# Hybrid decoder layer on one core: tile addresses at equal residues, and the order of five small steps

## The chip, the cores and the metric

One core of a Trainium2 chip runs the whole layer. The metric is the device time of one execution in microseconds (us). TensorE (PE) multiplies; VectorE (DVE), ScalarE (ACT) and GpSimd (POOL) compute; SyncE (SP), ACT and POOL also issue DMAs. Each engine takes its own instructions strictly in order.

## The reference

The input x has 1024 rows of 1024 float32. With h = RMSNorm(x)·g, one projection z = h·W_in (1024 x 6160) gives all branch inputs:

```
a_out = chunked_sgu(gelu(a_u), gelu(a_v), ...) * silu(a_gate)   # 8 groups of 128 channels
o     = gla_chunked(b_q, b_k, b_v, log_sigmoid(gate)/16)        # 4 heads, chunks of 64 rows
b_out = rmsnorm(o, per head) * silu(b_gate)
y     = concat(a_out, b_out) @ w_out                            # 2048 x 1024
return x + rmsnorm(y, post_g)
```

chunked_sgu normalizes its v over 1024 channels, multiplies each 128-row chunk by a lower triangular 128x128 matrix per group, adds a bias and multiplies by u.

## The kernel before

**Matrix products.** Every float32 operand of a large product is split into a rounded part hi and the rest lo (`split`, L104: a cast on ACT, a subtraction on DVE), and `mm3` (L108) makes three matmuls of each product: hi·hi, hi·lo, lo·hi. A matmul has a stationary operand of 128x128 and a moving one of 128x512 (128x256 in the attention). Two forms use the normalized, transposed h (tiles `hT`) and the weight granules (tiles `gr`): `proj_tok` (L170) moves the weights past a stationary piece of hT, in the trace `ps<-gr,hT`; `proj_col` (L180) moves hT past a stationary piece of weights, `ps<-hT,gr`. The output projection (`product`, L719) moves weights past the split left operands `ah` and `al`: `ps<-gr,ah`.

**Stages, in order of time.** (1) x is loaded, normalized and transposed by `prep` (L215) tile by tile, while `first_block` projects head 0's v and gate. (2) For the four heads, `qk` makes decayed q and k, and `attend` (L425 on) runs the gated linear attention by 128 rows. What follows an attend is put off by `later(fn, n)` and run at the n-th `tick` (one each 12 matmuls of a projection); so `out` (transposes of the finished og, L467, and its store to `mix_d`) stands with n = 3. (3) The first half and then the second half of a_v are projected and passed through Gelu and statistics (loop L543). Between the halves stand the transposes of the triangular matrices (L556), their copies `wsT` (L557) and their row sums (L562, a product with ones). (4) For 8 groups g: u and gate by `proj_col`, the spatial product (L589), and sums of W_out blocks by `wout_sums` (written to `wo_d`). (5) The output projection as seven products of halves (L764 to L799); the last one calls `done` for the post norm, the residual and the stores.

**What sets the order.** Tiles and waits come from a tile framework, which also orders each engine's instructions by a simulated timeline when the program is built; an edit in one place can shift neighbours. A pool hands out its buffers in turn and packs its tiles one behind the other, so a small tile shifts the start of all behind it.

**Addresses.** In the built program the byte address of each operand modulo 256 is the same for all matmuls of a kind: hT 224, gr 160, ah and al 160, attention v, st, qs and kst 96, sc 192, ident 128, h 160, wsT 224.

**Names.** `raw`: weights as loaded; `gain`: pre norm weights on all partitions, here made by two matmuls of ones with the row (L247 to L250); `first_a`: a part of mix_d read back for stage 5; `wb`, `wh`: the blocks of `wout_sums`.

Of the kernel before, what the change touches and what calls it, by code (L numbers as in the profile page):

```python
# [8 lines left out]
F32 = mybir.dt.float32  # L9
# [6 lines left out]
P = 128  # L16
# [17 lines left out]
def hybrid_layer(  # L34
# [55 lines left out]
    make_identity(nc, ident)  # L90
    neghalf = const.tile([P, 8], F32, name="neghalf")
    nc.vector.memset(neghalf, -0.5)

    def rsqrt(dst, mean, more=None):
        if more is None:
            nc.gpsimd.tensor_scalar(out=dst, in0=mean, scalar1=EPS, scalar2=None, op0=ALU.add)
        else:
            nc.vector.tensor_scalar(
                out=dst, in0=mean, scalar1=EPS, scalar2=more, op0=ALU.add, op1=ALU.add
            )  # L100
        nc.gpsimd.tensor_tensor(out=dst, in0=dst, in1=neghalf[:, : dst.shape[-1]], op=ALU.pow)
# [22 lines left out]

    def block_a(cols, before=lambda k2: None, fine=False):

        got = []
        for k2 in range(KT // 2):
            before(k2)
            raw = raw_tile([2, W])  # L130
            c = 0
            for c0, n in cols:
                nc.sync.dma_start(
                    raw[:, :, c : c + n],
                    w_in[k2 * 256 : (k2 + 1) * 256, c0 : c0 + n].rearrange("(k p) c -> p k c", p=P),
                )
                c += n
            hi, lo = granule([2, W])
            if fine:
                for j in range(2):  # L140
                    split(hi[:, j], lo[:, j], raw[:, j])
            else:
                split(hi, lo, raw)
            got += [(hi[:, j], lo[:, j]) for j in range(2)]
        return got

    def block_b(cols):
# [58 lines left out]
    with tc.tile_pool(name="pre", bufs=2) as pre:  # L206
# [45 lines left out]
        blk = block_a(  # L252
            ((C_BV, DV), (C_BG, DV)), lambda k2: load(1) if k2 == 2 else None, fine=True
        )
# [19 lines left out]
    with tc.tile_pool(name="gla", bufs=1) as gp:  # L274
# [21 lines left out]
        )  # L296
        ba = gp.tile([P, H], F32, name="ba")
        nc.gpsimd.dma_start(ba, b_a2.rearrange("(h p) -> p h", p=P))
# [35 lines left out]
        def gates(hd, hf):  # L334
# [36 lines left out]
            nc.scalar.activation(out=f, in_=f, func=AF.Exp, scale=1.0 / TAU)  # L371
            dec = gp.tile([P, 8, 1], F32, tag="dec", name="dec", bufs=2)
            nc.vector.tensor_copy(dec, b[:, :, CH - 1 : CH])
            dec2 = gp.tile([P, 4, 1], F32, tag="dec2", name="dec2", bufs=3)
            tt(out=dec2, in0=dec[:, 0::2], in1=dec[:, 1::2], op=ALU.mult)
# [49 lines left out]
        def attend(hd, t, got, v, sg, cur):  # L425
# [23 lines left out]
            if e == 0:  # L449
                cur["og"] = gp.tile([P, 2, DV], F32, tag="og", name="og", bufs=2)  # L450
                cur["oss"] = gp.tile([P, 2], F32, tag="oss", name="oss", bufs=2)
            og, oss = cur["og"], cur["oss"]
# [4 lines left out]
            if e == 1:  # L457
# [19 lines left out]

                later(out, 3)

# [39 lines left out]
    vn = [vnp.tile([P, NT, 256], F32, name=f"vn{j}") for j in range(4)]  # L519
    first_a = vnp.tile([P, 4, 4, P], F32, name="first_a")  # L520

    def mixed_a(g, hf):
        return vn[g // 2][:, 4 * hf : 4 * hf + 4, (g % 2) * P : (g % 2 + 1) * P]

    with tc.tile_pool(name="sgu", bufs=1) as sp_:
# [9 lines left out]
        )  # L535
        gb = sp_.tile([P, 2, G], F32, name="gb")
        nc.gpsimd.dma_start(gb[:, 0], ln_g.rearrange("(g p) -> p g", p=P))
# [5 lines left out]
        for i in range(2):  # L543
            if i == 1:
                blk = block_a(((C_V + 512, 512),))
            for t in range(NT):
                pv = pv_first[t] if i == 0 and t < 2 else proj_tok((t,), blk)[0]
                for j in range(2):
                    vt = vn[2 * i + j][:, t]
                    nc.scalar.activation(out=vt, in_=pv[:, j * 256 : (j + 1) * 256], func=AF.Gelu)  # L550
                    nc.vector.bn_stats(out=stats[:, t, 2 * i + j], in_=vt)
            if i == 0:
                for r in range(2):
                    pt = bank()
                    for g in range(4):
                        nc.tensor.transpose(pt[:, g * P : (g + 1) * P], wsr[:, 4 * r + g], ident)  # L556
                    nc.scalar.copy(  # L557
                        out=wsT[:, 4 * r : 4 * r + 4], in_=pt.rearrange("p (g c) -> p g c", g=4)
                    )
                for r in range(2):  # L560
                    pt = bank()
                    nc.tensor.matmul(  # L562
                        pt, ones, wsT[:, 4 * r : 4 * r + 4].rearrange("p g t -> p (g t)"),
                        start=True, stop=True,
                    )
                    for g in range(4 * r, 4 * r + 4):
                        nc.vector.scalar_tensor_tensor(
                            out=q[:, g], in0=pt[:, (g % 4) * P : (g % 4 + 1) * P],
                            scalar=gb[:, 1, g : g + 1], in1=q[:, g], op0=ALU.mult, op1=ALU.add,
                        )  # L570
        mv = sp_.tile([P, NT, 2], F32, name="mv")
        for t in range(NT):
            nc.vector.bn_aggr(out=mv[:, t], in_=stats[:, t].rearrange("p a b -> p (a b)"))
        rs = sp_.tile([P, NT, 1], F32, name="rs")
        rsqrt(rs.rearrange("p t o -> p (t o)"), mv[:, :, 1])
# [47 lines left out]
        for g in range(G):  # L623
# [7 lines left out]
            for i, func in enumerate((AF.Gelu, AF.Silu)):  # L631
                for hf in range(2):
# [28 lines left out]
    with tc.tile_pool(name="outp", bufs=1, side="right", reuse_waits="tile") as op:  # L661
        vtt = nc.vector.tensor_tensor
        pog = op.tile([P, D], F32, name="pog")
        nc.gpsimd.dma_start(pog, row_bc(post_g, D))
# [79 lines left out]
        y = [[op.tile([P, D], F32, name=f"y{hf}{t}") for t in range(4)] for hf in range(2)]  # L744
        sums = op.tile([P, 2, 4, 2], F32, name="sums")
        ss = [[sums[:, hf, t] for t in range(4)] for hf in range(2)]

# [5 lines left out]
        def finish(hf, t, xr, pieces):  # L753
            r = slice((4 * hf + t) * P, (4 * hf + t + 1) * P)
            rstd = op.tile([P, 1], F32, tag="rstd", name="rstd", bufs=2)
            rsqrt(rstd, ss[hf][t][:, 0:1], ss[hf][t][:, 1:2])
# [68 lines left out]
```

## Time and profile before

| | us |
|---|---|
| median of 3 runs (lowest, highest) | 813.18 (812.63, 816.85) |
| the profiled execution | 816.81 |
| its span, first to last instruction | 815.1 |
| PE busy in it | 786.8 (97%) |
| DVE, ACT, POOL busy | 415.6, 328.6, 129.2 |
| mean granted TensorE clock | 0.989 |

The page's line per engine gives busy time and share of the span. A busy PE is not a fast PE: a matmul's shown duration overlaps the next one's, so the pace is read from the distance between two starts. The granted clock is 1.0 at 2.4 GHz and 0.5 at 1.2 GHz. Idle time on an engine other than PE costs nothing unless PE waits for it.

### The profile page before, as it was taken

To read this page: it belongs to the slowest core of one execution; us is meant where nothing else is said; L and a number is where in the kernel's file an instruction comes from. 1 tells how busy PE (TensorE), PEld (TensorE's weight loads), DVE (VectorE), ACT (ScalarE), POOL (GpSimd) and SP (SyncE) were. 2 spreads that over 40 slices of the span, in tenths; PEclk is the share of its full clock that TensorE was granted. 3 is DMA by queue.
4 is the path that set the end of the run, shared out by engine and by line. 5 is a ranking of instruction groups with operands and counts; after the bars stand their busy time and mean duration, and the time that the engine had idled before them with its cause. 6 is when DMAs were issued, how large, how long until landed. Compare 5 with 4: busy or idle time off the path is not lost.

```text
span 815.1 us, 9989 instructions
## 1 busy us (share of the span) xinstructions
PE 786.8 (97%) x3776; PEld 644.6 (79%) x3776; DVE 415.6 (51%) x703; ACT 328.6 (40%) x589; POOL 129.2 (16%) x182
## 2 busy tenths in 40 slices
PE   5999999999899999999979999999999989999995
PEld 3888887888788878888858888888888878888884
DVE  5534589425552456252465586513333268534665
ACT  5536467326442644241333333323233243444431
POOL 1232234312321222112001011100000010000012
PEclk9999999999999999999989999999999999999998
DMA  9304011103010401034584765731110096344157
GB/s 282 115 2 116 4 50 53 52 27 110 27 52 2 136 27 52 1 124 136 207 257 169 222 218 192 243 119 52 53 53 27 26 358 261 132 154 153 52 188 276
DMA packets 62946, 97.33 MB, mean 119 GB/s; under 512 B 4849, under 2 KB 38641, under 8 KB 62898
## 3 DMA queue, kind: packets, MB, share of 16 engines
q1 hardware_dynamic: 54816, 68.76, 25.9%
q0 software_dynamic: 7504, 27.41, 9.5%
q8 instruction: 30, 0.49, 0.2%
q10 hardware_dynamic: 578, 0.53, 0.2%
q14 instruction: 18, 0.15, 0.1%
HBM read 71.51 MB, written 25.17 MB: 119 GB/s over the span
## 4 chain that ended last, share of the span: by engine, by line
PE 81%; DVE 5%; ACT 5%; DMA 4%; issue 3%; POOL 1%; SPq 0%; POOLq 0%; DVEq 0%; ACTq 0%
PE ps L111 25%; PE ps L112 25%; PE ps L113 25%; PE ps L589 2%; DMA raw<-in_w_in_dram 2%; ACT gr L105 1%; PE ps L321 1%; DMA wo_d<-wb 1%; PE ps L236 1%; DMA wsr<-in_a_w_s_dram 1%; PE ps L467 1%; DVE stl L106 1%; DVE b L355 1%; DVE og L460 1%; DVE y L758 1%
## 5 line engine op out<-in xcount | busy, mean ns | idle before, releaser
L111 PE MATMUL ps<-gr,hT 128*128 128x512 f32 x384 | 154.7, 405 | 0.0
L112 PE MATMUL ps<-gr,hT 128*128 128x512 f32 x384 | 152.9, 399 | 0.0
L113 PE MATMUL ps<-gr,hT 128*128 128x512 f32 x384 | 152.3, 398 | 0.0
L111 PE MATMUL ps<-hT,gr 128*128 128x512 f32 x384 | 152.2, 396 | 0.0
L113 PE MATMUL ps<-hT,gr 128*128 128x512 f32 x384 | 151.6, 396 | 0.0
L112 PE MATMUL ps<-hT,gr 128*128 128x512 f32 x384 | 151.4, 394 | 0.0
L106 DVE TENSOR_TENSOR gr<-raw,gr 128x1024 fp32r<-128x1024 f32 (+1 forms) x64 | 73.3, 1154 | 33.8 <-ACT gr L105 33.8
L111 PE MATMUL ps<-gr,ah 128*128 128x512 f32 x224 | 87.3, 390 | 2.1 <-ACT ah L105 2.1
L112 PE MATMUL ps<-gr,ah 128*128 128x512 f32 x224 | 87.0, 389 | 0.0
L111 PEld LDWEIGHTS ps<-gr,hT 128*128 128x128 f32 x384 | 73.1, 190 | 16.9 <-issue 0.5
L113 PEld LDWEIGHTS ps<-gr,hT 128*128 128x128 f32 x384 | 73.0, 190 | 16.6
L112 PEld LDWEIGHTS ps<-gr,hT 128*128 128x128 f32 x384 | 73.0, 190 | 16.2 <-issue 0.5
L113 PE MATMUL ps<-gr,al 128*128 128x512 f32 x224 | 85.8, 389 | 0.0
L112 PEld LDWEIGHTS ps<-hT,gr 128*128 128x128 f32 x384 | 72.7, 189 | 15.7
L113 PEld LDWEIGHTS ps<-hT,gr 128*128 128x128 f32 x384 | 72.7, 189 | 15.4
L111 PEld LDWEIGHTS ps<-hT,gr 128*128 128x128 f32 x384 | 73.0, 190 | 15.0
L105 ACT CAST gr<-raw 128x1024 fp32r<-128x1024 f32 (+1 forms) x64 | 62.9, 992 | 44.1 <-PE ps L113 28.2
L635 ACT ACTIVATE u<-ps 128x512 f32<-128x512 f32 x32 | 19.1, 598 | 86.9 <-PE ps L113 86.9
L590 DVE SCALAR_TENSOR_TENSOR vn<-ps,gb,q 128x512 f32<-128x512 f32 x16 | 12.0, 747 | 79.1 <-PE ps L589 79.1
L111 PEld LDWEIGHTS ps<-gr,ah 128*128 128x128 f32 x224 | 42.1, 188 | 11.3 <-ACT ah L105 2.6
L113 PEld LDWEIGHTS ps<-gr,al 128*128 128x128 f32 x224 | 42.1, 188 | 8.8
L112 PEld LDWEIGHTS ps<-gr,ah 128*128 128x128 f32 x224 | 42.1, 188 | 8.6
(191 smaller groups left out, 1032.6 us busy)
## 6 DMA issues: line engine op xcount, KB each, us to landing
raw<-in_w_in_dram SPq DMA_DIRECT2D x80, 256.0 KB, 4.0
gr<-wo_d SPq DMA_DIRECT2D x16, 1024.0 KB, 4.8
wb<-in_w_out_dram SPq DMA_DIRECT2D x32, 256.0 KB, 3.8
wo_d<-wh POOLq DMA_DIRECT2D x8, 1024.0 KB, 4.7
wo_d<-wb POOLq DMA_DIRECT2D x8, 1024.0 KB, 6.5
raw<-in_w_out_dram SPq DMA_DIRECT2D x12, 512.0 KB, 3.9
mix_d<-mixB POOLq DMA_DIRECT2D x8, 512.0 KB, 3.2
raw<-in_w_in_dram SPq DMA_DIRECT2D x8, 512.0 KB, 3.6
```

The costliest lines, as they stand in the source:

```text
L105: nc.scalar.copy(out=hi, in_=src)
L106: (eng or nc.vector).tensor_tensor(out=lo, in0=src, in1=hi.bitcast(F32), op=ALU.subtract)
L111: nc.tensor.matmul(ps, a[0], b[0], start=start, stop=False, **how)
L112: nc.tensor.matmul(ps, a[0], b[1], start=False, stop=False, **how)
L113: nc.tensor.matmul(ps, a[1], b[0], start=False, stop=stop, **how)
L236: nc.tensor.transpose(pt[:, k * P : (k + 1) * P], h[:, kk * P : (kk + 1) * P], ident)
L321: nc.tensor.matmul(pl, w_lr[k // 4][:, k % 4], part, start=(k == 0 and i == 0), stop=(k == KT - 1 and i == 1),)
L355: nc.vector.tensor_tensor_scan(out=b.rearrange("p n c -> p (n c)"), data0=seg, data1=mf, initial=0.0, op0=ALU.mult, op1=ALU.add,)
L460: nc.vector.tensor_scalar_mul(og[:, i], og[:, i], oss[:, i : i + 1])
L589: nc.tensor.matmul(pt[:, c], part[:, c], wsT[:, g], start=True, stop=True)
L590: nc.vector.scalar_tensor_tensor(out=part, in0=pt, scalar=gb[:, 0, g : g + 1], in1=q[:, g : g + 1].to_broadcast([P, 4, P]), op0=ALU.mult, ...
L635: nc.scalar.activation(out=u, in_=pu.rearrange("p (c t) -> p c t", c=4), func=func)
```

## The change

It has these parts:

1. Tile sizes. Small tiles are widened to 32 floats (128 bytes) or given another shape, and two tiles of 56 floats that nobody uses are put into the pools `hp` and `outp`. The arithmetic is the same. The residues modulo 256 are then hT 0, gr 0, ah and al 0, v, st, qs and kst 0, sc 128, ident 128, h 0, wsT 128.
2. Start. `gain` comes by one DMA that reads the row for each partition; the two matmuls and copies go. The first two weight granules are loaded from ACT's queue (`early=2`), not SP's.
3. `rsqrt` with two sums does its addition on POOL, not on DVE.
4. `out` of a head's last tile is put off by 4 ticks, not 3.
5. The transposes and copies of the triangular matrices stand after tile 4 of the first a_v half, the row sums after tile 2 of the second, in the program's text.
6. The first two left operands of the output projection are split earlier, into tiles of their own (`ready_a`).
7. The last block's rows are stored in two pieces, not three.

```diff
-    neghalf = const.tile([P, 8], F32, name="neghalf")
+    LINE = 32
+    neghalf = const.tile([P, LINE], F32, name="neghalf")
...
-            nc.vector.tensor_scalar(
+            nc.gpsimd.tensor_scalar(
                 out=dst, in0=mean, scalar1=EPS, scalar2=more, op0=ALU.add, op1=ALU.add
...
-                nc.sync.dma_start(
+                (nc.scalar if k2 < early else nc.sync).dma_start(
                     raw[:, :, c : c + n],
...
+    hp.tile([P, 56], F32, name="pad")
...
-            ss = pre.tile([P, 2], F32, tag="ss", name="ss", bufs=3)
+            ss = pre.tile([P, LINE], F32, tag="ss", name="ss", bufs=3)
...
-        g_row = pre.tile([1, D], F32, name="g_row", bufs=1)
-        nc.scalar.dma_start(g_row, pre_g.rearrange("(o n) -> o n", o=1))
-        one = pre.tile([1, P], F32, name="one", bufs=1)
-        nc.vector.memset(one, 1.0)
-        for j in range(2):
-            pt = bank()
-            nc.tensor.matmul(pt, one, g_row[:, j * W : (j + 1) * W], start=True, stop=True)
-            nc.vector.tensor_copy(gain[:, j * W : (j + 1) * W], pt)
+        nc.sync.dma_start(gain, row_bc(pre_g, D))
...
-                later(out, 3)
+                later(out, 4 if t == NT - 1 else 3)
...
+    ready_a = [tuple(vnp.tile([P, 4, P], F32R, name=f"ra{i}{j}") for i in "hl") for j in range(2)]
...
-            if i == 0:
-                for r in range(2):
+                if (i, t) == (0, 4):
+                    for r in range(2):
...
+                if (i, t) == (1, 2):
+                    for r in range(2):
+                        pt = bank()
+                        nc.tensor.matmul(
+                            pt, ones, wsT[:, 4 * r : 4 * r + 4].rearrange("p g t -> p (g t)"),
...
+                        if g == 7:
+                            for j in range(2):
+                                split(*ready_a[j], first_a[:, j])
...
-                a = tuple(op.tile([P, 4, P], F32R, tag="a" + i, name="a" + i, bufs=6) for i in "hl")
-                split(*a, left(j, l))
+                if l == "a11" and j < 2:
+                    a = ready_a[j]
+                else:
...
+        op.tile([P, 56], F32, name="pad")
...
-            finish(1, t, xrs[t], (C1, slice(0, 256), slice(256, W)))
+            finish(1, t, xrs[t], (C1, C0))
```

Three places show how the built order moves. First, PE at the start of a head's q and k (stage 2): `og` is the finished attention of the head before, `lrT` the next gates' product. Before:

```order
L113 MATMUL ps<-hT,gr 128x512
L467 MATMUL ps<-ident,og 128x128 x2
L337 MATMUL ps<-lrT,w_512 128x512
L111 MATMUL ps<-hT,gr 128x512
L112 MATMUL ps<-hT,gr 128x512
```

and of the change:

```order
L115 MATMUL ps<-hT,gr 128x512
L333 MATMUL ps<-lrT,w_504 128x512
L113 MATMUL ps<-hT,gr 128x512
...
L114 MATMUL ps<-hT,gr 128x512
L115 MATMUL ps<-hT,gr 128x512
L463 MATMUL ps<-ident,og 128x128 x4
```

The transposes of og move behind the gates' product and 12 matmuls, all four together. (For the last head, which has no gates behind it, 27 matmuls stood ahead of the second pair and 32 stand ahead of the four.)

Second, ACT at the end of the first a_v half (stage 3); `vn` is Gelu's output, `wh` the rounded W_out sums. Before:

```order
L105 CAST wh<-wb 128x1024
L550 ACTIVATE vn_3275<-ps 128x256
L550 ACTIVATE vn_3276<-ps 128x256
L105 CAST wh<-wb 128x1024
L105 CAST gr<-raw 128x1024 x3
L550 ACTIVATE vn_3275<-ps 128x256
L550 ACTIVATE vn_3276<-ps 128x256
L557 COPY wsT<-ps 128x512 x2
```

and of the change:

```order
L107 CAST rah_3265<-first_a 128x512
L107 CAST rah_3267<-first_a 128x512
L547 ACTIVATE vn_3260<-ps 128x256
L547 ACTIVATE vn_3261<-ps 128x256
L554 COPY wsT<-ps 128x512 x2
L547 ACTIVATE vn_3260<-ps 128x256
L547 ACTIVATE vn_3261<-ps 128x256
L107 CAST wh<-wb 128x1024
L547 ACTIVATE vn_3260<-ps 128x256
L547 ACTIVATE vn_3261<-ps 128x256
L107 CAST wh<-wb 128x1024
L107 CAST gr<-raw 128x1024 x3
```

The copies of wsT now stand ahead of the casts of wh; the casts of the second half's weights (gr) still stand behind them. The early casts `rah` of the left operands stand here too. On PE the row sums are placed behind the first three matmuls of the second half.

Third, DVE at the start of the program. Before:

```order
L98 TENSOR_SCALAR ss<-ss 128x1
L250 COPY gain<-ps 128x512
L230 SCALAR_TENSOR_TENSOR h<-xt,ss,gain 128x512
L106 TENSOR_TENSOR gr<-raw,gr 128x512 x2
L250 COPY gain<-ps 128x512
L106 TENSOR_TENSOR gr<-raw,gr 128x512 x2
L230 SCALAR_TENSOR_TENSOR h<-xt,ss,gain 128x512
L106 TENSOR_TENSOR hT<-ps,hT 128x4x128
```

and of the change:

```order
L94 MEMSET neghalf 128x32
L108 TENSOR_TENSOR gr<-raw,gr 128x512 x2
L233 SCALAR_TENSOR_TENSOR h<-xt,ss,gain 128x512 x2
L108 TENSOR_TENSOR hT<-ps,hT 128x4x128
L233 SCALAR_TENSOR_TENSOR h<-xt,ss,gain 128x512 x2
L108 TENSOR_TENSOR gr<-raw,gr 128x512 x2
```

Both halves of the first h now stand behind one granule's subtractions, not behind two and a copy from PSUM.

## Rows read from the trace of the kernel before

**Rows 1.** The page's line of busy time by engine.

```profile
PE 786.8 (97%) x3776; PEld 644.6 (79%) x3776; DVE 415.6 (51%) x703; ACT 328.6 (40%) x589; POOL 129.2 (16%) x182
```

**Rows 2.** Groups of PE by form: count; busy us, mean ns; idle before.

```profile
L111 PE MATMUL ps<-gr,hT 128*128 128x512 f32 x384 | 154.7, 405 | 0.0
L111 PE MATMUL ps<-hT,gr 128*128 128x512 f32 x384 | 152.2, 396 | 0.0
L111 PE MATMUL ps<-gr,ah 128*128 128x512 f32 x224 | 87.3, 390 | 2.1 <-ACT ah L105 2.1
```

**Rows 3.** Timeline of PE, three unbroken stretches: start us, duration us, what.

```profile
36.90 0.40 PE L112 MATMUL ps<-gr,hT 128*128 128x512 f32 x1
...
42.03 0.39 PE L113 MATMUL ps<-gr,hT 128*128 128x512 f32 x1
...
529.64 0.39 PE L111 MATMUL ps<-hT,gr 128*128 128x512 f32 x1
...
545.88 0.39 PE L113 MATMUL ps<-hT,gr 128*128 128x512 f32 x1
...
801.04 0.39 PE L113 MATMUL ps<-gr,al 128*128 128x512 f32 x1
...
806.48 0.39 PE L113 MATMUL ps<-gr,al 128*128 128x512 f32 x1
```

**Rows 4.** Waits of PE: who for whom, us in total, times, longest.

```profile
PE ps L236 <- DVE h L230: 6.2, 2, 5.2
PE ps L467 <- DVE og L460: 4.2, 2, 2.3
PE ps L562 <- ACT wsT L557: 4.1, 1, 4.1
PE ps L111 <- ACT ah L105: 2.1, 1, 2.1
```

**Rows 5.** Stretches: us, busy of PE, PEld, DVE, ACT, POOL, clock, DMA.

```profile
206.66:210.07 3.41, 3.37 (x9) 2.79 (x10) 1.93 (x5) 0.62 (x1) 0.71 (x1) 0.50 0.00 0
...
411.46:418.29 6.83, 6.06 (x10) 3.51 (x11) 4.93 (x12) 1.20 (x3) 0.00 (x0) 0.50 1.00 323
```

**Rows 6.** Timeline of ACT at 204 us.

```profile
204.69 0.37 ACT L453 ACTIVATE og<-ps 128x256 f32<-128x256 f32 x1
```

**Rows 7.** Timeline of PE, ACT and DVE from 374 to 418 us.

```profile
374.85 0.38 PE L467 MATMUL ps<-ident,og 128*128 128x128 f32 x2
...
405.77 1.05 ACT L105 CAST wh<-wb 128x1024 fp32r<-128x1024 f32 x1 [9.07 <-issue]
...
409.98 3.49 DVE L106 TENSOR_TENSOR gr<-raw,gr 128x1024 fp32r<-128x1024 f32 x3
...
412.23 3.78 PE L562 MATMUL ps<-wsT,ones 128*128 128x512 f32 x4 [4.15 <-ACT wsT L557]
...
416.23 0.63 PE L112 MATMUL ps<-gr,hT 128*128 128x512 f32 x1
...
417.94 0.56 PE L113 MATMUL ps<-gr,hT 128*128 128x512 f32 x1
```

**Rows 8.** Timeline of ACT at the start of the output projection.

```profile
649.39 1.05 ACT L105 CAST gr<-raw 128x1024 fp32r<-128x1024 f32 x1 [3.95 <-PE ps L113]
...
653.57 2.18 ACT L105 CAST ah<-first_a 128x512 fp32r<-128x512 f32 x4
```

**Rows 9.** Timeline of ACT, DVE and PE at the program's start.

```profile
8.85 1.14 ACT L105 CAST gr<-raw 128x512 fp32r<-128x512 f32 x2 [3.63 <-DMA raw<-in_w_in_dram]
...
10.71 0.68 DVE L250 COPY gain<-ps 128x512 f32<-128x512 f32 x1
...
14.08 0.78 PE L111 MATMUL ps<-gr,hT 128*128 128x512 f32 x1
```

**Rows 10.** Timeline of DVE and ACT's queue at the program's end.

```profile
810.39 1.54 DVE L758 SCALAR_TENSOR_TENSOR y<-y,rstd,xr 128x512 f32<-128x512 f32 x3 [0.72 <-POOL rstd L101]
...
808.58 3.33 ACTq L762 DMA_DIRECT2D out_dram<-y  x2
```

More of the change, by code (lines that the diff above doesn't have):

```diff
@@ L123, in raw_tile, with block_a @@
         return wts.tile([P] + shape, F32, tag="raw", name="raw", bufs=3)
-    def block_a(cols, before=lambda k2: None, fine=False):
+    def block_a(cols, before=lambda k2: None, fine=False, early=0):
         got = []
@@ L242, in hybrid_layer @@
         gain = pre.tile([P, D], F32, name="gain", bufs=1)
-        g_row = pre.tile([1, D], F32, name="g_row", bufs=1)
-        nc.scalar.dma_start(g_row, pre_g.rearrange("(o n) -> o n", o=1))
-        one = pre.tile([1, P], F32, name="one", bufs=1)
-        nc.vector.memset(one, 1.0)
-        for j in range(2):
-            pt = bank()
-            nc.tensor.matmul(pt, one, g_row[:, j * W : (j + 1) * W], start=True, stop=True)
-            nc.vector.tensor_copy(gain[:, j * W : (j + 1) * W], pt)
+        nc.sync.dma_start(gain, row_bc(pre_g, D))
         prep(0)
         blk = block_a(
-            ((C_BV, DV), (C_BG, DV)), lambda k2: load(1) if k2 == 2 else None, fine=True
+            ((C_BV, DV), (C_BG, DV)), lambda k2: load(1) if k2 == 2 else None, fine=True, early=2
         )
@@ L296, in hybrid_layer @@
         )
-        ba = gp.tile([P, H], F32, name="ba")
+        ba = gp.tile([P, LINE], F32, name="ba")[:, 0:H]
         nc.gpsimd.dma_start(ba, b_a2.rearrange("(h p) -> p h", p=P))
@@ L371, in gates @@
             nc.scalar.activation(out=f, in_=f, func=AF.Exp, scale=1.0 / TAU)
-            dec = gp.tile([P, 8, 1], F32, tag="dec", name="dec", bufs=2)
+            dec = gp.tile([P, LINE, 1], F32, tag="dec", name="dec", bufs=2)[:, 0:8]
             nc.vector.tensor_copy(dec, b[:, :, CH - 1 : CH])
-            dec2 = gp.tile([P, 4, 1], F32, tag="dec2", name="dec2", bufs=3)
+            dec2 = gp.tile([P, LINE, 1], F32, tag="dec2", name="dec2", bufs=3)[:, 0:4]
             tt(out=dec2, in0=dec[:, 0::2], in1=dec[:, 1::2], op=ALU.mult)
@@ L450, in attend @@
                 cur["og"] = gp.tile([P, 2, DV], F32, tag="og", name="og", bufs=2)
-                cur["oss"] = gp.tile([P, 2], F32, tag="oss", name="oss", bufs=2)
+                cur["oss"] = gp.tile([P, LINE], F32, tag="oss", name="oss", bufs=2)[:, 0:2]
             og, oss = cur["og"], cur["oss"]
@@ L535, in hybrid_layer @@
         )
-        gb = sp_.tile([P, 2, G], F32, name="gb")
+        gb = sp_.tile([P, 4, G], F32, name="gb")
         nc.gpsimd.dma_start(gb[:, 0], ln_g.rearrange("(g p) -> p g", p=P))
@@ L551, in hybrid_layer @@
                     nc.vector.bn_stats(out=stats[:, t, 2 * i + j], in_=vt)
-            if i == 0:
-                for r in range(2):
[L554 to L569, printed above, removed]
-                        )
@@ L571, in hybrid_layer @@
-        mv = sp_.tile([P, NT, 2], F32, name="mv")
+                if (i, t) == (0, 4):
+                    for r in range(2):
+                        pt = bank()
+                        for g in range(4):
+                            nc.tensor.transpose(pt[:, g * P : (g + 1) * P], wsr[:, 4 * r + g], ident)
+                        nc.scalar.copy(
+                            out=wsT[:, 4 * r : 4 * r + 4], in_=pt.rearrange("p (g c) -> p g c", g=4)
+                        )
+                if (i, t) == (1, 2):
+                    for r in range(2):
+                        pt = bank()
+                        nc.tensor.matmul(
+                            pt, ones, wsT[:, 4 * r : 4 * r + 4].rearrange("p g t -> p (g t)"),
+                            start=True, stop=True,
+                        )
+                        for g in range(4 * r, 4 * r + 4):
+                            nc.vector.scalar_tensor_tensor(
+                                out=q[:, g], in0=pt[:, (g % 4) * P : (g % 4 + 1) * P],
+                                scalar=gb[:, 1, g : g + 1], in1=q[:, g], op0=ALU.mult, op1=ALU.add,
+                            )
@@ L572, in hybrid_layer @@
+        mv = sp_.tile([P, NT, 4], F32, name="mv")[:, :, 0:2]
         for t in range(NT):
             nc.vector.bn_aggr(out=mv[:, t], in_=stats[:, t].rearrange("p a b -> p (a b)"))
-        rs = sp_.tile([P, NT, 1], F32, name="rs")
+        rs = sp_.tile([P, LINE, 1], F32, name="rs")[:, 0:NT]
         rsqrt(rs.rearrange("p t o -> p (t o)"), mv[:, :, 1])
@@ L662, in hybrid_layer @@
         vtt = nc.vector.tensor_tensor
+        small = op.tile([P, 4 * LINE], F32, name="small")
         pog = op.tile([P, D], F32, name="pog")
@@ L724, in product @@
                     b = right(j, r)
-                a = tuple(op.tile([P, 4, P], F32R, tag="a" + i, name="a" + i, bufs=6) for i in "hl")
-                split(*a, left(j, l))
+                if l == "a11" and j < 2:
+                    a = ready_a[j]
+                else:
+                    a = tuple(op.tile([P, 4, P], F32R, tag="a" + i, name="a" + i, bufs=6) for i in "hl")
+                    split(*a, left(j, l))
                 held.append((j, a, b[j % 2]))
@@ L744, in hybrid_layer @@
         y = [[op.tile([P, D], F32, name=f"y{hf}{t}") for t in range(4)] for hf in range(2)]
-        sums = op.tile([P, 2, 4, 2], F32, name="sums")
-        ss = [[sums[:, hf, t] for t in range(4)] for hf in range(2)]
+        ss = [[small[:, 8 * hf + 2 * t : 8 * hf + 2 * t + 2] for t in range(4)] for hf in range(2)]
         def residual(hf, t):
@@ L754, in finish @@
             r = slice((4 * hf + t) * P, (4 * hf + t + 1) * P)
-            rstd = op.tile([P, 1], F32, tag="rstd", name="rstd", bufs=2)
+            rstd = small[:, 16 + 4 * hf + t : 17 + 4 * hf + t]
             rsqrt(rstd, ss[hf][t][:, 0:1], ss[hf][t][:, 1:2])
```

## The prediction

> **What bounds the kernel now.** I read the page's busy line first: PE is busy for 97% of the span, every other engine for about half or less [rows 1]. So time can go in two ways only: PE takes its matmuls at a closer pace, or one of the few gaps of PE closes. A busy time doesn't tell the pace, because the records overlap; the view that tells it is the timeline of PE, where I took the distance of two starts in stretches without a wait. Three forms make up 2976 of the 3776 matmuls: weights moving past h (384 records in each of the three lines of `mm3`, so 1152), h moving past weights (1152), and the output projection (672) [rows 2]. Their starts are 233.2 ns apart (22 intervals from 36.90 to 42.03), 228.7 ns (71 intervals from 529.64 to 545.88) and 226.7 ns (24 intervals from 801.04 to 806.48; rounded up to 227 below) [rows 3]. All have 512 columns, the same clock and the same kind of operands. What differs is the residue of the addresses: in the third form moving and stationary tile have 160 and 160, in the first two 160 and 224. The view of waits gives the gaps: 6.2 us for h, 4.2 for og, 4.1 for wsT, 2.1 for ah [rows 4]. The view by windows adds what a gap costs behind it: stretches in which the granted clock is 0.50 [rows 5].
>
> **(a) Residues.** The two projection forms get the equality that the output projection has (0 and 0). If equality is what makes 227 ns, they gain 1152 x (233.2 - 227.0) = 7.1 us and 1152 x (228.7 - 227.0) = 2.0 us, together 9.1. About 0.8 is lost again: between 374.85 and 405.77 PE runs some 30.9/0.2332 = 132 matmuls while a cast on ACT waits for a chain that PE doesn't shorten (below, c); 132 x 6.2 ns there end in a longer wait. I take **8.3**. The output projection stays at equal residues and is put at no change. The other 800 matmuls (attention, transposes, gates) are put at nothing, since they are short and end mostly on other engines. Bounds: 0 if the residue has no part in it; and on the other side the closest pace that a row shows, 4 intervals of 427 ns at half clock from 416.23 to 417.94, so 214 ns of columns at full clock [rows 7].
>
> **(b) og.** Before, PE reaches the transposes of og at the start of a head's q and k, 2.3 us at most ahead of og's copies: 2 waits, 4.2 us in all [rows 4]; the chain that makes og ends on ACT at 204.69 for the first of them and is not changed [rows 6]. Each wait is followed by a stretch of 3.41 us at clock 0.50, one at 206.66 [rows 5] and one of the same length at 292; work of 3.41 us at half clock is 1.7 at full, so 1.7 is lost each time. Of the change, the transposes stand behind the gates' product and 12 matmuls, 12 x 0.229 + 0.4 = 3.2 us, more than 2.3. The wait goes, and with no pause ahead the clock should hold: 4.2 + 2 x 1.7 = **7.6**. Late next would be the pieces of q and k for the same head, some 3 us further on; I see none within 1.5 us. Bounds: 3 (the clock falls nevertheless and a rest of the waits stays) to 7.6.
>
> **(c) Row sums.** The wait for wsT of 4.1 us goes from its place: its copies now stand ahead of the casts of `wh` on ACT. But PE needs something else right then, the second half's weights, whose casts stay behind those of `wh`. The cast at 405.77 was held for 9.07 us by nothing that the engines show [rows 7]: it waits for a block that is loaded, written and loaded again through DMA, begun when PE passes og's last transposes at 374.85. That chain takes 30.9 us and, as those transposes now come 5 matmuls later (1.2 us), it ends later against PE. From it the first gr is cast and DVE's subtraction, which began at 409.98, gives the lo part. So PE's second matmul of the half, which came at 416.23, comes at about 412.3: 3.9 us earlier. The row sums, which took 3.78 us for four at half clock [rows 7], stand now behind the third matmul and cost about 3.4 there. Net **0.5**; the new wait on gr, about 4 us, keeps the stretch at 0.50 of 6.83 us [rows 5] as it is. Bounds: -2 (the chain is later still) to 4.1 + 6.83/2 = 7.5 (all of the wait and the slow clock go).
>
> **(d) Left operands.** Stage 5 opened with a wait of 2.1 us for ah [rows 4], four casts from 653.57 behind the cast of gr at 649.39 [rows 8]. The first two operands are now cast back in stages 3 and 4. Then only gr holds PE, which is there at 649.39 + 1.05, and the third operand is needed only after 24 x 0.227 = 5.4 us. **2.1**; bounds 0 to 2.1.
>
> **(e) Start.** The first projection matmul is at 14.08; its hT hangs on h, and h on `gain`, whose first half DVE copies from PSUM at 10.71 in 0.68 us [rows 9]. The two copies leave DVE's queue, and one pair of subtractions no longer stands ahead of the second half of h: with 3.49/3 us for 1024 columns [rows 7], so 0.58 for 512, this is 2 x 0.68 + 2 x 0.58 = **2.5**. How long the broadcast DMA takes no row shows; it has the size of one x tile. The weights for which ACT's cast at 8.85 waited 3.63 us [rows 9] bound the load from below: where `gain` lands by about 10 us, it is covered. ACT now issues the two weight loads in front of its first squares, which costs something too. Bounds: -1 (gain lands 3.5 us late) to 5.
>
> **(f) End.** Each 128-row tile of the last block was finished by three products, 1.54 us in all, the last one from 810.39, and stored in pieces of 3.33/2 = 1.7 us of ACT's queue [rows 10]. Two pieces for three save 1.54/3 = 0.5 and part of one store, 1.0 by choice: **1.5**. The addition of `rsqrt` on POOL costs about what DVE's did. Bounds 0 to 2.5.
>
> **Sum.** 8.3 + 7.6 + 0.5 + 2.1 + 2.5 + 1.5 = 22.5 us. Against the profiled execution: 816.81 - 22.5 = 794.3. That one lies 3.6 above the median of 813.18, so against the median **790.7**. Its own range is 783 to 797: upwards (b) and (c) at their bad ends would give 4.6 + 2.5 = 7.1, of which I take 6, since both at once are unlikely; downwards (c) at its good end gives 7.0.
>
> **Rivals.**
>
> R1, residues do nothing. The three forms differ in more than residues: which tile moves, which engine writes it, how much DMA runs beside. Against it: gr moves in the first and the third form, and the stationary operand alone sets 233 apart from 227 [rows 3]. For it: I have no third residue that would show a pace of its own. Then 8.3 goes and the rest stays: 799 (797 to 803, the latter with 4.1 of (b) lost too). The Trainium skill, "SBUF — State Buffer", section "Who interferes with whom", says that PE has one read port for the moving operand and an independent one for loading weights, and that PE never waits on anyone; by that rule the two operands can't disturb each other and R1 is right. The rows' 6 ns between two forms with the same moving tile speak against it.
>
> R2, the residue 0 itself is what counts, not the equality. Then the output projection, which goes from 160 to 0, gains as well. By the bound of 214 to 218 ns [rows 7], the three forms save 9 to 13 ns on each of 2976 matmuls, 27 to 39 us on top of the forecast: 752 to 764, and with half of the smaller saving 777. Against it: the rows at 214 are at half clock, and no row at full clock is under 226. The Trainium skill, "TensorE: Matmul & The Clock Gate", section "Wait — 56ns, not 53.3ns?", gives 215.7 ns between matmuls of 512 columns at the full clock; by that figure all forms carry an excess of 11 to 17 ns here, and removing the 11 that are left at 227 would give 790.7 - 2.976 x 11.3 = 757 as an estimate.
>
> R3, slower: operands that start at the same residue meet in memory. Both read streams begin in the same place at each matmul, and what is 227 at 160 becomes worse at 0. The other five steps give 14.2; with the 2976 matmuls at an average of 230.1 before, the point from which this decides is 230.1 + 14.2/2.976 = 235 ns. At 238 ns the matmuls cost 7.9 x 2.976 = 23.5 more, so 813.2 + 23.5 - 14.2 = 822. For it: nothing but that the first form shows that 233 can occur. Against it: the third form, equal and the closest of all.
>
> R4, the waits only move: PE runs ahead of DMA-bound chains in stages 3 and 4, og and gr are late by as much as PE came earlier, and 809 to 813 remains.
>
> **How the numbers follow.** Forecast 0.58, R1 0.20, R2 0.10, R3 0.06, R4 0.06. About 0.5% (4.1 us) is what a measurement of this kernel can tell from no change. R1 and R2 are faster but for 0.02 of R1; with the forecast: 0.86 faster. Within: 0.06 of R4 and that 0.02, so 0.08. Slower: R3, 0.06. The range takes the forecast's 783 to 797, R1 up to 803 and the near end of R2 down to 777; outside are most of R2, R3 and R4, about 0.2.
>
> **What would show it.** Starts of both projection forms 227 ns apart, the output projection unchanged (under 220: R2; 229 and 233 as before: R1; over 235: R3). No wait of PE for og and no 0.50 stretch behind 204 and 289. The row sums without a wait, but a wait of about 4 us for gr at the second half, and the slow stretch behind it. First projection near 11.5 us; no wait for ah in stage 5; about 6.5 us from the last matmul to the end. I am wrong if the pace moves otherwise than 227, or if the gaps named come back as waits for other operands.

## The result, and the profile after

The changed kernel was measured twice. The first time its four executions took 790.95, 793.71 and twice 4433 us; in the profile of one of these two the granted clock reads 1.00 throughout, and yet the matmuls of 512 columns start 1.28 to 1.45 us apart. No later execution of any kernel was like them, and their cause is not known. The four executions of the second time are what everything here rests on. These gave a median of 792.94 us (791.95 to 794.26), against 813.35 for the kernel before on the same chip: a ratio of 0.9746, interval 0.9727 to 0.9765, so 20.7 us less (19.1 to 22.2). The forecast was 790.7, range 777 to 803. The profiled execution took 791.95 us.

The page's span and busy line, and below it the view of PE's waits (who for whom, us in total, times, longest), of the changed kernel:

```profile
span 789.9 us, 9961 instructions
PE 768.8 (97%) x3772; PEld 640.1 (81%) x3772; DVE 411.2 (52%) x687; ACT 328.7 (42%) x589; POOL 139.9 (18%) x191
...
PE ps L239 <- DVE h L233: 10.5, 1, 10.5
PE ps L113 <- ACT gr L107: 2.3, 1, 2.3
PE ps L114 <- DVE stl L108: 0.7, 1, 0.7
PE ps L113 <- ACT hT L107: 0.6, 1, 0.6
```

The waits for og, wsT and ah of [rows 4] are gone. One for gr of 2.3 us is new. The wait for h is longer only on paper: the matmuls with `one` and the transposes of the first half of h, which stood in between, are no longer there.

The timeline of PE in the changed kernel (start us, duration us, what), one unbroken stretch of each projection form, and the first and last matmul of each:

```profile
36.00 0.39 PE L113 MATMUL ps<-gr,hT 128*128 128x512 f32 x1
...
39.86 0.39 PE L115 MATMUL ps<-gr,hT 128*128 128x512 f32 x1
...
508.26 0.39 PE L113 MATMUL ps<-hT,gr 128*128 128x512 f32 x1
...
529.11 0.39 PE L115 MATMUL ps<-hT,gr 128*128 128x512 f32 x1
```

17 intervals in 3.86 us are 227.1 ns, where [rows 3] had 233.2; 92 intervals in 20.85 us are 226.6 ns, where it had 228.7. A matmul's own shown duration, 0.39 us, is nearly what it was: the pace stands between two starts.

The windows of the changed kernel (stretch us; length, busy us of PE, PEld, DVE, ACT, POOL; clock, DMA share, GB/s), two at the places of the slow stretches behind og, and the one that is left:

```profile
200.00:203.41 3.41, 3.41 (x18) 2.81 (x17) 3.16 (x11) 1.27 (x4) 0.94 (x2) 1.00 0.00 0
282.00:285.41 3.41, 3.41 (x19) 2.80 (x18) 1.93 (x5) 1.11 (x2) 0.71 (x1) 1.00 0.00 0
395.30:398.71 3.41, 3.39 (x6) 2.07 (x7) 3.41 (x4) 2.42 (x4) 0.82 (x2) 0.50 0.83 308
```

At the second a_v half, the timelines of POOL, SP, DVE, ACT and PE of the changed kernel read:

```profile
376.41 0.75 POOL L615 DMA_DIRECT2D wo_d<-wb  x1 [0.47 <-DVE wb L108]
385.98 1.76 SPq L601 DMA_DIRECT2D wb<-in_w_out_dram  x4
389.71 0.69 DVE L606 TENSOR_TENSOR wb<-wb 128x512 f32<-128x512 f32 x1 [6.39 <-DMA wb<-in_w_out_dram]
391.78 1.05 ACT L107 CAST wh<-wb 128x1024 fp32r<-128x1024 f32 x1 [8.98 <-DVE wb L606]
394.21 2.95 ACT L107 CAST gr<-raw 128x1024 fp32r<-128x1024 f32 x3
395.32 1.65 PE L113 MATMUL ps<-gr,hT 128*128 128x512 f32 x3 [2.34 <-ACT gr L107]
396.76 2.85 PE L560 MATMUL ps<-wsT,ones 128*128 128x512 f32 x4
```

This is the chain that the forecast described: the first block is written out from 376.41, the second block's loads are issued at 385.98, ACT waits for them, and the cast of gr stands behind it. At the start, and at the end:

```profile
6.79 1.29 DVE L108 TENSOR_TENSOR gr<-raw,gr 128x512 fp32r<-128x512 f32 x2 [5.84 <-ACT gr L107]
9.67 1.41 DVE L233 SCALAR_TENSOR_TENSOR h<-xt,ss,gain 128x512 f32<-128x512 f32 x2 [1.59 <-DMA gain<-in_pre_norm_g_dram]
13.01 0.80 PE L113 MATMUL ps<-gr,hT 128*128 128x512 f32 x1 [0.56 <-ACT hT L107]
...
784.18 0.30 POOL L100 TENSOR_SCALAR small<-small 128x1 f32<-128x1 f32 x1 [1.75 <-ACT junk L744]
785.16 1.41 DVE L762 SCALAR_TENSOR_TENSOR y<-y,small,xr 128x512 f32<-128x512 f32 x2 [0.36 <-POOL small L103]
```

The subtractions of gr are over by 8.08 and DVE then waits for `gain`. The last products run from 785.16, 1.9 us behind the last matmul's end (783.30); in [rows 10] they began at 810.39, 3.5 behind it (806.87). From there to the end it is 4.7 us in both. What came earlier is the addition of `rsqrt`: it now runs on POOL at 784.18, right behind ACT's sum; in the kernel before it stood in DVE's queue behind the products of the tile before, which run from 807.40 to 808.94, and so began only at 809.46:

```profile
807.40 1.54 DVE L758 SCALAR_TENSOR_TENSOR y<-y,rstd,xr 128x512 f32<-128x512 f32 x3 [0.72 <-POOL rstd L101]
...
809.46 0.20 DVE L98 TENSOR_SCALAR rstd<-sums 128x1 f32<-128x1 f32 x1
```

To compare the parts, the table gives when four milestones came in the profiled executions (start us; the last column is span minus the end of the last matmul). The second and third row are experiments told below.

| kernel | first projection | stage 4 | output projection | end | tail |
|---|---|---|---|---|---|
| before | 14.08 | 461.74 | 654.24 | 815.05 | 8.18 |
| before + residues | 14.91 | 453.78 | 644.56 | 806.80 | 7.99 |
| changed, old residues | 13.13 | 448.60 | 638.80 | 797.87 | 6.56 |
| changed | 13.01 | 442.34 | 630.82 | 789.85 | 6.55 |

### The profile page after: what moved, and what is told of

Read it like the earlier page. It is cut to its first block, busy times and chain, and to the rows that moved or that the text cites. A ratio compares the mean times of both kernels' runs of the same rounds, so it can differ in the third digit from the quotient of the medians.

```text
span 4431.7 us, 9961 instructions
## 1 busy us (share of the span) xinstructions
PE 4414.4 (100%) x3772; PEld 3130.3 (71%) x3772; DVE 416.4 (9%) x687; ACT 336.2 (8%) x589; POOL 130.5 (3%) x191
## 4 chain that ended last, share of the span: by engine, by line
PE 100%; DMA 0%; DVE 0%; SPq 0%; DVEq 0%; POOLq 0%; issue 0%; ACTq 0%; POOL 0%; ACT 0%
PE ps L114 31%; PE ps L115 31%; PE ps L113 31%; PE ps L587 2%; PE ps L463 1%; PE ps L239 1%; PE ps L317 1%; PE ps L402 1%; PE ps L412 1%; PE ps L404 0%; PE ps L560 0%; PE ps L333 0%; DMA gain<-in_pre_norm_g_dram 0%; PE ps L403 0%; PE ps L553 0%; SPq L216 0%
## 5 line engine op out<-in xcount | busy, mean ns | idle before, releaser
L113 PE MATMUL ps<-gr,hT 128*128 128x512 f32 x384 | 657.8, 1719 | 0.0
L113 PE MATMUL ps<-hT,gr 128*128 128x512 f32 x384 | 656.0, 1708 | 0.0
L114 PE MATMUL ps<-hT,gr 128*128 128x512 f32 x384 | 651.4, 1696 | 0.0
L115 PE MATMUL ps<-hT,gr 128*128 128x512 f32 x384 | 650.1, 1695 | 0.0
L115 PE MATMUL ps<-gr,hT 128*128 128x512 f32 x384 | 649.9, 1697 | 0.0
L114 PE MATMUL ps<-gr,hT 128*128 128x512 f32 x384 | 648.9, 1695 | 0.0
L115 PEld LDWEIGHTS ps<-hT,gr 128*128 128x128 f32 x384 | 351.0, 914 | 155.5 <-issue 155.1
L115 PEld LDWEIGHTS ps<-gr,hT 128*128 128x128 f32 x384 | 351.1, 914 | 147.4 <-issue 146.4
L114 PEld LDWEIGHTS ps<-hT,gr 128*128 128x128 f32 x384 | 350.6, 913 | 147.6 <-issue 147.6
L113 PEld LDWEIGHTS ps<-hT,gr 128*128 128x128 f32 x384 | 349.5, 910 | 147.2 <-issue 147.2
L113 PEld LDWEIGHTS ps<-gr,hT 128*128 128x128 f32 x384 | 350.1, 912 | 146.3 <-issue 145.7
L114 PEld LDWEIGHTS ps<-gr,hT 128*128 128x128 f32 x384 | 351.2, 915 | 140.4 <-issue 140.2
L113 PE MATMUL ps<-gr,ah 128*128 128x512 f32 x216 | 366.1, 1695 | 0.0
L114 PE MATMUL ps<-gr,ah 128*128 128x512 f32 x216 | 365.7, 1693 | 0.0
L115 PE MATMUL ps<-gr,al 128*128 128x512 f32 x216 | 364.4, 1694 | 0.0
L113 PEld LDWEIGHTS ps<-gr,ah 128*128 128x128 f32 x216 | 197.3, 914 | 88.4 <-issue 88.4
L114 PEld LDWEIGHTS ps<-gr,ah 128*128 128x128 f32 x216 | 197.3, 914 | 88.2 <-issue 88.2
L115 PEld LDWEIGHTS ps<-gr,al 128*128 128x128 f32 x216 | 197.4, 914 | 88.0 <-issue 68.8
L587 PEld LDWEIGHTS ps<-wsT,vn 128*128 128x128 f32 x128 | 88.9, 938 | 6.4 <-issue 6.4
L587 PE MATMUL ps<-wsT,vn 128*128 128x128 f32 x128 | 87.4, 1046 | 0.0
```

The source lines that it names most:

```text
L113: nc.tensor.matmul(ps, a[0], b[0], start=start, stop=False, **how)
L114: nc.tensor.matmul(ps, a[0], b[1], start=False, stop=False, **how)
L115: nc.tensor.matmul(ps, a[1], b[0], start=False, stop=stop, **how)
L587: nc.tensor.matmul(pt[:, c], part[:, c], wsT[:, g], start=True, stop=True)
```

## The experiments

**The changed kernel again.** No edit.

> The changed kernel once more, with its profile. Forecast: 790.7 us (783 to 797), starts of both projection forms 227 ns apart, no wait of PE for og, no stretch of clock 0.50 behind 204 and 289, a wait of about 4 us on gr at the second a_v half, first projection near 11.5 us. If the residues do nothing: 797 to 803, with 233 and 229 ns as before.

792.94 us, the profile above. The time, the pace, og and its slow stretches came as said; the wait for gr was 2.3 us and not 4, the first projection came at 13.0 and not 11.5.

**The residues alone, and all but the residues.** The first is the kernel before with the tile sizes of the diff, the second the changed kernel with the old sizes; the core of both edits, in the first's direction:

```diff
+hp.tile([P, 56], F32, name="pad")
...
-ss = pre.tile([P, 2], F32, tag="ss", name="ss", bufs=3)
+ss = pre.tile([P, LINE], F32, tag="ss", name="ss", bufs=3)
...
```

> The kernel before with the tile sizes of part 1 alone (all residues as in the changed kernel, no other part). Forecast: 8.3 us less than the kernel before, about 805 (803 to 807), 227 ns in both projection forms. If the residues do nothing: 813 and 233 and 229 ns. If equal residues at 0 collide: over 820.

> The changed kernel with the old tile sizes (residues hT 224, gr 160, ah and al 160 again), all other parts kept. Forecast: 790.7 + 8.3 = 799 (797 to 801), 233 and 229 ns. If the residues do nothing: the same time as the changed kernel. If the parts help each other (PE pauses less, so the clock holds): more than 801.

With the residues alone 807.77 us (ratio 0.9920, 0.9897 to 0.9944), so 6.5 less by the ratio (4.6 to 8.4); the median is 0.8 above the range that was expected. With all but the residues 799.67 us; the residues are then worth 799.67 - 792.94 = 6.7, and in the profiled spans 797.87 - 789.85 = 8.0. Over the intervals of the two forms at full clock and without a wait, the mean was 227.6 and 227.4 ns with the new residues, 233.3 and 229.2 with the old, whatever the other parts. In the first kernel part of the gain may have come back as waiting: the wait for wsT, behind a chain through DMA, was 5.5 us, against 4.1, 5.0 and 4.8 in three profiles of the kernel before.

**Eight residues in one run.** Eight pairs of left operands at eight residues, in turn, in the output projection:

```diff
+NB, GAP, turn = 8, [8] * 8, [0]
...
-a = tuple(op.tile([P, 4, P], F32R, tag="a" + i, name="a" + i, bufs=6) for i in "hl")
+n = turn[0] % NB
+turn[0] += 1
+a = tuple(op.tile([P, 4, P], F32R, tag=f"a{i}{n}", name=f"a{i}{n}", bufs=1) for i in "hl")
+if turn[0] <= NB and GAP[n]:
+    op.tile([P, GAP[n]], F32, name=f"gap{n}")
```

> The changed kernel with eight pairs of left operands in the output projection, each pair 32 bytes further modulo 256 than the one before (stationary at 0, 32, ... 224, moving gr at 0), in turn. It shows the pace against the difference of the residues. Equality theory: 227 ns at 0, more at others, and near 229 to 233 at 64 and 192. Theory that another thing than the residue differs between the forms: 227 ns at all eight. Theory of a whole line of 64 bytes: 0, 64, 128 and 192 alike, and 32, 96, 160, 224 alike and slower. Whole time as the changed kernel, up to 672 x 7/8 x 6 ns = 3.5 us more.

The timeline of PE in this kernel. Each row is the first of 12 matmuls whose stationary operand is at residue 0, 32, 64, 96, 128, 160, 192 and 224, in this order; the last row begins the next round at 0. The moving operand is at 0 throughout:

```profile
662.41 0.39 PE L113 MATMUL ps<-gr,ah 128*128 128x512 f32 x1
...
665.14 0.39 PE L113 MATMUL ps<-gr,ah 128*128 128x512 f32 x1
...
667.93 0.40 PE L113 MATMUL ps<-gr,ah 128*128 128x512 f32 x1
...
670.73 0.39 PE L113 MATMUL ps<-gr,ah 128*128 128x512 f32 x1
...
673.53 0.39 PE L113 MATMUL ps<-gr,ah 128*128 128x512 f32 x1
...
676.31 0.39 PE L113 MATMUL ps<-gr,ah 128*128 128x512 f32 x1
...
679.12 0.40 PE L113 MATMUL ps<-gr,ah 128*128 128x512 f32 x1
...
681.87 0.40 PE L113 MATMUL ps<-gr,ah 128*128 128x512 f32 x1
...
684.67 0.39 PE L113 MATMUL ps<-gr,ah 128*128 128x512 f32 x1
```

The distances divided by 12 are 227.5, 232.5, 233.3, 233.3, 231.7, 234.2, 229.2 and 233.3 ns, and the other rounds repeat them. Only equality gives 227. Each residue always meets the same place in a product here; in the changed kernel, where all eight places have residue 0, each of them has 226.7, so the place is not what counts. The two old forms fall on the right places: a stationary operand 64 further than the moving one (224 against 160) had 233, one 64 less (192 here) had 229. The theory of whole lines of 64 bytes falls with 64 and 128. From the output projection's first matmul to the program's last one, 155.41 us against 152.09: 3.3 more, where up to 3.5 was expected. The whole run, one execution, took 799.01, since its wait for gr was 4.1 us this time and the slow stretch behind it 6.83:

```profile
PE ps L113 <- ACT gr L107: 4.1, 1, 4.1
...
397.15:403.98 6.83, 6.00 (x10) 3.45 (x11) 6.83 (x13) 3.24 (x5) 1.51 (x2) 0.50 0.77 264
```

Up to there this program is the changed kernel's. What differs is DMA: DVE waits 18.5 us for the loads of the two blocks wb here, 15.6 in the changed kernel's profile.

**og's transposes at 3 ticks again**, twice:

```diff
-later(out, 4 if t == NT - 1 else 3)
+later(out, 3)
```

> The changed kernel with the transposes of og put off by 3 ticks again, in front of the gates' product; all else kept. Theory: the two waits for og come back (about 2 us each) and with each a stretch of granted clock 0.50 of some 3.41 us right behind it: about 7 us more than the changed kernel, 800 (798 to 801). Rival: the waits come back but the clock stays at 1.0, since the slow stretches had another cause: 4 us more, 797. Rival: the chain that makes og ends earlier in the changed kernel by itself, no wait comes back: 793.

> The changed kernel with og's transposes put off by 3 ticks, one more execution with its profile. Theory: waits of 4.0 us for og again, with none, one or two stretches of 0.50 behind them, and the time moves by 1.7 us for each. Rival: in the changed kernel something else keeps the clock up; none again.

798.13 us, 5.2 more than the changed kernel (5.8 by the ratios to the kernel before, as the two were measured on different chips), and 797.41 in the single execution. The view of waits and the windows right behind the two waits, of the first:

```profile
PE ps L463 <- DVE og L456: 4.0, 2, 2.1
...
203.00:206.41 3.41, 2.94 (x16) 2.45 (x16) 2.30 (x7) 0.62 (x1) 0.31 (x2) 1.00 0.00 0
284.80:288.21 3.41, 3.00 (x16) 2.49 (x16) 2.30 (x6) 0.62 (x1) 0.34 (x1) 1.00 0.00 0
```

The waits are back, the slow stretches are not, in either execution: this is the rival's case. From the start of the gates' projection to the last matmul of the first a_v half it is 4.7 and 4.8 us more than in the changed kernel's profile, which is what the waits are worth. Whether something in the changed kernel keeps the clock up, the second rival, these runs don't decide.

**The kernel before, two more profiles.** No edit.

> The kernel before, unchanged, one more execution with its profile. Its first profile (816.81 us, 3.6 over the median) had a stretch of clock 0.50 of 3.41 us behind each of the two waits for og; the changed kernel with these waits put back had none. Theory: after a pause of PE of about 2 us the slow stretch comes in some executions and not in others, 1.7 us each, so the place of an execution in the spread of 812 to 817 us follows from it: waits of 2 us again, fewer than two stretches behind them, and about 1.7 us less for each that is missing. Rival: the stretches belong to the program: both are there again, at whatever time.

> The same as the run before it, a third execution of the kernel before with its profile. Theory: the number of slow stretches behind og's waits differs among the three profiles while the waits stay at 4.2 us. Rival: two in each.

815.29 and 817.18 us. Waits for og and the windows behind them, of the second profile and then of the third:

```profile
PE ps L467 <- DVE og L460: 3.7, 2, 2.0
...
206.80:210.21 3.41, 3.18 (x16) 2.66 (x17) 2.12 (x6) 0.62 (x1) 0.52 (x1) 1.00 0.00 0
289.50:292.91 3.41, 3.17 (x16) 2.65 (x17) 2.13 (x6) 0.62 (x1) 0.52 (x1) 1.00 0.00 0
```

```profile
PE ps L467 <- DVE og L460: 3.7, 2, 1.9
...
206.94:210.35 3.41, 3.41 (x10) 2.73 (x10) 1.71 (x5) 0.62 (x1) 0.93 (x1) 0.50 0.00 0
290.60:294.01 3.41, 3.16 (x16) 2.64 (x17) 2.14 (x6) 0.62 (x1) 0.50 (x1) 1.00 0.00 0
...
654.09:657.50 3.41, 3.41 (x9) 2.65 (x8) 2.34 (x4) 0.68 (x2) 0.00 (x0) 0.50 0.99 369
```

Two slow stretches behind og in the first profile, none in the second, one in the third, behind pauses of 1.7 to 2.3 us (none behind one of 1.99, one behind one of 1.92). So the program alone doesn't set their number. From the start of the gates' projection to the last matmul of the first a_v half the three profiles take 346.1, 342.5 and 344.0 us: there the time does follow, by 1.6 to 2.1 us for each stretch. The second half of the expectation, that the whole time follows from their number, is not borne out: the third execution has one fewer there, but one behind the wait for ah, and is no faster; the second is 1.5 faster than the first with two fewer, as its gates' projection began 0.9 later and its wait for wsT was 0.8 longer.

**Two buffers for wb.**

```diff
-b = sp_.tile([P, 4, W], F32, tag="wb", name="wb")
+b = sp_.tile([P, 4, W], F32, tag="wb", name="wb", bufs=2)
...
```

> The changed kernel with two buffers for wb in place of one (mv and rs in their old, smaller shapes, to make room). The second block's load then waits for no write of the first block. Theory: the wait of PE for gr at the second a_v half (2.3 us in one execution, 4.1 in another) is set by the chain load, write, load through DMA; it goes or falls under 1 us, and the stretch of clock 0.50 behind it goes or shrinks: 789 to 791, and less spread between executions. Rival: the casts of gr are held by the buffers that PE frees at the end of the first half, not by this chain: unchanged, 793.

790.65 us (789.81 to 791.48), 0.9720 of the kernel before (0.9702 to 0.9737): all four executions are faster than the changed kernel's four of the second time (0.9746, 0.9727 to 0.9765, on another chip), though one is slower than its 790.95 of the first time. By the times alone the 2 us are not beyond doubt; the trace shows where they come from. ACT, PE and the window there:

```profile
381.43 2.00 ACT L107 CAST wh<-wb 128x1024 fp32r<-128x1024 f32 x2 [1.03 <-DVE stats L548]
388.88 1.05 ACT L107 CAST gr<-raw 128x1024 fp32r<-128x1024 f32 x1 [0.70 <-PE ps L115]
...
392.76 0.85 PE L113 MATMUL ps<-gr,hT 128*128 128x512 f32 x3
393.44 1.88 PE L560 MATMUL ps<-wsT,ones 128*128 128x512 f32 x4
...
396.84 0.50 PE L114 MATMUL ps<-gr,hT 128*128 128x512 f32 x1 [1.05 <-DVE gr L108]
...
392.76:399.59 6.83, 5.78 (x22) 3.81 (x21) 5.85 (x9) 3.86 (x5) 0.00 (x0) 1.00 0.37 102
```

The second block's casts of wh run at 381.43 and not 391.78, the first cast of gr comes 5.3 us earlier, and the first wait and the slow stretch are gone; a wait of 1.05 on the lo part is left. The row sums take 1.88 us, not 2.85, as they run at full clock. The rival falls: PE frees the buffer early enough.

**gain in two halves.**

```diff
-nc.sync.dma_start(gain, row_bc(pre_g, D))
+for j in range(2):
+    c = slice(j * W, (j + 1) * W)
+    nc.sync.dma_start(gain[:, c], row_bc(pre_g[c], W))
```

> The changed kernel with the broadcast of the pre norm row in two loads of 256 KB, one for each half, on the same queue at the same place. Theory: the first h waits 1.6 us for the landing of gain alone; the first half lands earlier, and the first projection comes near 11.5 to 12 us (13.01 now): 791 to 792. Rival: the start is bound by all DMA together (300 GB/s in the first 20 us), the halves land no earlier: 793 and 13.0.

793.93 us, first projection at 12.87, the gates' projection at 59.07 (59.09 in the changed kernel): a miss. The first half of h did come earlier, at 9.05 and not 9.67, but ACT then held hT back, DVE's wait for gain staying at 1.75 us:

```profile
9.05 0.75 DVE L233 SCALAR_TENSOR_TENSOR h<-xt,ss,gain 128x512 f32<-128x512 f32 x1 [1.75 <-DMA gain<-in_pre_norm_g_dram]
...
11.20 1.14 ACT L107 CAST gr<-raw 128x512 fp32r<-128x512 f32 x2 [4.10 <-DMA raw<-in_w_in_dram]
12.24 0.58 ACT L107 CAST hT<-ps 128x512 fp32r<-128x512 f32 x1
```

ACT's next cast of gr waits for weights until 11.20, and the cast of hT is behind it. The new order and the load's size changed together, so it stays open which of both decides.

**(d) and (f) undone.** With them goes the addition of `rsqrt`, back to DVE:

```diff
-nc.gpsimd.tensor_scalar(
+nc.vector.tensor_scalar(
...
-if g == 7:
-    for j in range(2):
-        split(*ready_a[j], first_a[:, j])
...
-if l == "a11" and j < 2:
-    a = ready_a[j]
...
-finish(1, t, xrs[t], (C1, C0))
+finish(1, t, xrs[t], (C1, slice(0, 256), slice(256, W)))
```

> The changed kernel with steps (d) and (f) undone, which lie 150 us apart: the first two left operands are cast at the start of the output projection again, the last block's rows go in three pieces, and the addition of rsqrt is DVE's. Theory: 2.1 us more at the start of the output projection, 1.6 more after the last matmul: 796.6 (795.5 to 798). Rival for (d): the wait is for gr's cast as well, so nothing is lost there: 794.5.

796.92 us, with 796.6 expected. The wait for ah is 2.1 us again, and the output projection begins 2.1 later (632.89 against 630.82); the tail is 7.99 us against 6.55. The rival falls. As the pieces and the addition went together, this run doesn't part the two.

## Why the prediction was right

The total fell within the forecast's own range, 2.2 us over its middle. The waits for og, wsT and ah and the pace moved as described, but the closeness of the sum is partly luck: by the medians (b) was put 2.4 us too high, and (c) was put 2.5 too low. Term by term, from the profiled executions:

| step | forecast | measured | from |
|---|---|---|---|
| (a) residues | 8.3 | 8.0 | spans with and without them; 6.7 by medians |
| (b) og | 7.6 | 8.3, 4.7 and 6.2, with two, no and one slow stretch | gates' projection to the end of the first a_v half: 346.1, 342.5 and 344.0 in three profiles of the kernel before, 337.8 in the changed kernel at the old pace |
| (c) row sums | 0.5 | 3.0 | last matmul of the first a_v half to stage 4: 53.9, now 50.9 at the old pace |
| (d) left operands | 2.1 | 2.1 | undone |
| (e) start | 2.5 | 1.8 | start of the gates' projection 61.68 to 59.89 at the old pace |
| (f) end | 1.5 | 1.6 | tail 8.18 to 6.55 |

With the 8.3 of the first profile they add up to 24.8, of a span that fell by 815.05 - 789.85 = 25.2. The medians fell by less, 20.7. By them (a) is 6.7, (b) put back 5.2, (d) and (f) undone 4.0; the 4.8 that are left for (c) and (e) are what the profiles show for these two.

(a) was right, and its reason is shown rather than argued: equal residues give 227 ns, seven other differences 229 to 234. R1 and R2 are out. R1 had a rule of the Trainium skill behind it, "SBUF — State Buffer", section "Who interferes with whom": PE reads the moving operand and loads weights through independent ports and never waits on anyone. The 6 ns measured between operands that differ only in an address don't agree with it, and the measurement decides. R2 needed the output projection to gain; it has 226.7 ns at 160 and 160 (the kernel with the old residues) and 226.7 at 0 and 0. R3 is out by the same number: at equal residues nothing is slower. R4 is out as well: of 10.4 us of waiting for og, wsT and ah, 2.3 came back as a wait for gr.

(b) removed both waits, as worked out, and they are worth 4.7. But "with no pause ahead the clock should hold", priced at 3.4 us, took two slow stretches of one profile for a property of the kernel. Of the 12 pauses of about 2 us for og in six profiles with them, 4 were followed by one: 4 of 8 in the kernel before, with and without the new residues, and none of 4 in the changed kernel with the waits put back. Whether the stretch would come there as often is open.

The sum took these 3.4 us off the median of other executions. Without them the forecast would have been 794. Whether the 3.6 us by which the first profile lay above the median were the same two stretches is not shown: a second profile without any took 815.29 us, 2.1 above that median, on another chip.

(c) was the term that was mis-sized: 0.5 for 3.0. The mechanism is the one described, and the experiment with two wb buffers shows it, since it cuts the chain. What failed is "a new wait on gr, about 4 us, keeps the stretch at 0.50 of 6.83 us": the wait was 2.3 us and the stretch 3.41. This too differs between executions: with eight residues, where the order up to there is the same, the wait was 4.1 and the stretch 6.83, and it was 52.7 us to stage 4, against 49.7 in the changed kernel's profile and 53.1 in the old order at the same pace (the residues alone). There nearly nothing of the gain is left, as forecast; in the four other profiles with this order (og put back twice, gain in halves, (d) and (f) undone) it was 48.4 to 49.9.

(e) misread a row: the copy at 10.71 in [rows 9] is the second half's. The first half's ran at 5.39, and DVE then stood idle for 2.58 us before the next subtractions, so its 0.68 could not be gained:

```profile
5.39 0.68 DVE L250 COPY gain<-ps 128x512 f32<-128x512 f32 x1
...
9.50 1.29 DVE L106 TENSOR_TENSOR gr<-raw,gr 128x512 fp32r<-128x512 f32 x2 [2.58 <-ACT gr L105]
```

The condition that it named, that gain land by about 10 us, held: it landed at 9.67. But DVE was free at 8.08, and the first projection came at 13.0. The first matmul gained 1.1, not 2.5; another 0.7 came up to the gates' projection. Against the two other profiles of the kernel before (62.54 and 62.08) the gates' projection gained 2.7 and 2.2.

(f) has the right size for another reason. The forecast looked for it in two products for three and in part of a store, and put the addition on POOL at nothing; but from the start of the last products to the end nothing was gained (4.7 us in both), and all of the 1.6 lies ahead of them, in the chain from the last sum to the products. How much of it is the addition's new place, and how much that the products of the tile before were two and not three, no run parts.

## What to carry to other kernels

Read a matmul's pace between two starts, by pair of operands, and look at the operands' byte addresses modulo 256: moving and stationary tiles at equal residues cost some widened tiles and two of padding, and gave 2 to 6 ns in 230 here. Before a term read from one profiled execution is taken off a median, see in a second and third profile whether it is there as well. Here a slow stretch of the clock came behind some pauses of about 2 us and not behind others; price the pause by its length, and the clock by how often the stretch comes in several profiles. And where a term comes out right, look whether the time was gained where the forecast said.

## What was not expected of the hardware

What counts is equality modulo 256, not 512: in the built programs the two operands of the output projection lie 256 apart modulo 512 in the kernel before, and 0 apart in the changed one, and both have 226.7 ns.

The residue that counts seems to be that of the next matmul's weights. At the borders of the groups in the run with eight residues, the matmul at 0 ahead of one at 32 took 235.0 ns to the next start (mean of 7), the one at 224 ahead of one at 0 took 226.7 (mean of 6): there the pace follows the next stationary operand, not the present one. The six other borders (229.0 to 237.0 ns) decide nothing: two lie within 0.5 ns of the present operand's mean, four near neither mean. These are few intervals, worked out from the record of the trace, and no run was made for them alone. At equal residues 227 ns remain, 13 more than the 214 that the 427 at half clock in [rows 7] would be at full clock; what they are no run shows.
